# Four-layer hybrid decoder trunk on one core: some low weight parts by an accumulating DMA, and conditioning tiles dealt anew

## The chip, the cores and the metric

The program runs on one core of a Trainium2 chip. The metric is the device time of one execution in microseconds (us), lower is better. TensorE multiplies matrices (PE in the profile, PEld for its weight loads), VectorE (DVE) and ScalarE (ACT) work on tiles element by element, GpSimd (POOL) fills constants and can issue DMAs, SyncE (SP) issues nearly all DMAs, in the order of its queue.

## What is computed

One sequence of 256 tokens, 1024 wide, passes four layers. Each layer is a token mixer and a gated feed-forward network; both sit behind a normalization that is shifted and scaled by six vectors per layer, made from one conditioning vector `c`.

```python
for i in range(4):
    mod = silu(c) @ ada_w[i] + ada_b[i]                  # 6 x 1024
    sh1, sc1, g1, sh2, sc2, g2 = split(mod, 6)
    h = rmsnorm(x, mix_norm_g[i]) * (1 + sc1) + sh1
    y = [gmlp, mla, hgrn2][i % 3](h)                     # layers 0 and 3: gMLP, 1: attention, 2: recurrence
    x = x + (1 + g1) * y
    h = rmsnorm(x, ffn_norm_g[i]) * (1 + sc2) + sh2
    a = h @ w_up                                         # 1024 x 5632
    gate, val = split(causal_conv3(a) + conv_b, 2)
    x = x + (1 + g2) * ((silu(gate) * val) @ w_down)     # 2816 x 1024
return rmsnorm(x, final_g)
```

All inputs are float32. The recurrence (layer 2) projects `h` to a forget gate f, a query q, a value i and an output gate g, each 1024 wide, and to an output o.

## The kernel before

**Weights.** Every weight passes once through SBUF, in units of 1 MB (128 partitions x 2048 floats, tile `raw`, a ring of five). A unit is converted in two halves of 1024 columns: ACT copies the half to a rounded high part `wh` (L214), DVE subtracts it from the raw half to get the low part `wl` (L217); seven halves of each are held. Activations are split in the same way (`hh` and `hlo` behind a norm, `gh` and `gl` in the feed-forward network). Each product is three matmuls: high x high, high x low, low x high.

`unit()` is called where a stage takes its next weight unit. It first issues the DMAs of coming units, then converts as far ahead as it should: three units as a rule, two in the out-projections, and three again at an out-projection's last unit, so that the first two units behind a norm are converted ahead of the norm (`LAST = 3`). `state["chain"]` puts later conversions behind the norm's own chain.

**A norm between two stages.** The end of an out-projection (`dn` of the feed-forward network, `go` of gMLP, `wo` of the others) is `out_end`: DVE multiplies by the gate (`early`, then four times `gated`, L541) and adds to `x` (L542), ACT sums squares, a root and a reciprocal follow, `gx` is the scaled `x` (L477, L480, L481). PE turns it into `xt` (L489), ACT and DVE make `hh` (L503) and `hlo` (L510, L514) with the shift and scale of the conditioning (`mod`, `amul`). `early` is put behind the last low part that DVE has made (`state["sub"]`) and behind the last conditioning tile on DVE.

**Conditioning.** `mod` of a layer has six parts (l, u): u = 0, 1, 2 are shift, scale and gate of the mixer, 3, 4, 5 those of the feed-forward network. The first two parts of layer 0 are made at the start. The other 22 are dealt to two engines, each part as four 1 MB tiles `adaw` (name: layer, part, quarter). Those in `ADA_P` are sixteen-pass matmuls on PE into `adaps` (L331), which DVE transposes and stores (`adat` L298, `mod` L300, `amul` L266); those in `ADA_D` are two DVE reductions a tile (L356). `RATE` gives for each stage how many tiles of PE and of DVE are loaded per weight unit. `GAPS` and `GAPRUN` say how many tiles for PE are held ready for a norm and are run there, where PE has little else; `HGF` is the number run in the recurrence's out-projection. `need()` runs what a norm or a gate cannot do without. Loads go through SP's queue, among those of the weights; the tiles for DVE and some of those for PE take slots of the `raw` ring.

**Order.** Each engine works through its own queue in order. The order is a scheduler's, made from the program order, priorities and `issue_after`.

Of the kernel before, what the change touches and what calls it, by code (L numbers as in the profile page):

```python
# [8 lines left out]
F32 = mybir.dt.float32  # L9
# [4 lines left out]
ALU = mybir.AluOpType  # L14
# [6 lines left out]
L = 4  # L21
# [3 lines left out]
NF = 22  # L25
GI = 2048
NRAW = 5
GAPS = [2, 4, 3, 3, 1, 2, 2, 0]
GAPRUN = [2, 2, 3, 3, 1, 2, 2]
GAPW = 7  # L30
GAPBIG = 3
LAST = 3
# [9 lines left out]
OLAG = 1  # L42
ROPE = 1
MLA_ADA = (2, 4, 6)
HGF = 2
HGO = "o0 o1 s0 a0 o2 s1 a1 n0 o3 s2 n1 w0 s3 n2 w1 n3 w2 w3"
HOLD = (3, 4)
ADA_P = [(0, 5), (1, 2), (1, 3), (2, 2), (2, 3), (2, 4), (3, 5)]
ADA_D = [(0, 2), (0, 3), (0, 4), (1, 0), (1, 1), (1, 4), (1, 5), (2, 0), (2, 1), (2, 5), (3, 0), (3, 1), (3, 2), (3, 3),
         (3, 4)]  # L50
RATE = {("mix", 0): (0.05, 0.9), ("u", 0): (0.1, 0.8), ("go", 0): (0.35, 0.6), ("up", 0): (0.1, 0.23),
        ("dn", 0): (0.0, 0.65), ("mix", 1): (2.0, 0.0), ("up", 1): (0.0, 0.2), ("dn", 1): (0.0, 0.85),
        ("mix", 2): (0.0, 0.0), ("lev", 2): (0.5, 0.0), ("hout", 2): (0.25, 0.0), ("up", 2): (0.0, 0.2),
        ("dn", 2): (0.0, 0.8), ("mix", 3): (0.0, 0.6), ("u", 3): (0.0, 0.5), ("go", 3): (0.0, 0.7),
        ("up", 3): (0.0, 0.0), ("dn", 3): (0.0, 0.0)}
MAGIC = 12582912.0
TWO_PI = 2.0 * math.pi
# [35 lines left out]
def build(ctx, tc, A, out, stages=None):  # L93
    nc = tc.nc
    pe, act, dve, pool = nc.tensor, nc.scalar, nc.vector, nc.gpsimd
# [60 lines left out]
    i = act.activation(cact[:], cin[:], AF.Silu)  # L156
# [12 lines left out]

    plan = []  # L170

    def want(aps):
        plan.extend(aps)

    state = {"dma": 0, "conv": 0, "use": 0, "ahead": 3, "chain": (), "behind": (), "manual": False, "left": 99, "tag": "raw", "p": 0.0, "d": 0.0, "gap": 0, "rate": {"p": 0.0, "d": 0.0}}
    raws = []
# [1 line left out]
    halves = []  # L178

    def dma_next():  # L180
        ap, n = plan[state["dma"]]
        raw = wp.tile([P, 2048], F32, tag="raw", name=f"raw{state['dma']}", bufs=NRAW)
        state["dma"] += 1
        if state["dma"] == 1:

            nc.sync.dma_start(raw[:, :1024], ap[:, :1024])
            raw_, ap = raw[:, 1024:], ap[:, 1024:]
        else:
            raw_ = raw[:, :n]
        i = nc.sync.dma_start(raw_, ap)  # L190
        state["lastdma"] = getattr(i, "ins", i)
        raws.append((raw, n))

    def conv_half():

        if not halves:
            if state["dma"] == state["conv"]:
                if state["dma"] == len(plan):
                    return
                dma_next()  # L200
            raw, n = raws.pop(0)
            ready.append([])
            halves.extend((raw, o, min(1024, n - o), state["conv"]) for o in range(0, n, 1024))
            state["conv"] += 1
        raw, o, w, n = halves.pop(0)
        wh = wp.tile([P, 1024], F32R, tag="wh", name=f"wh{n}_{o}", bufs=7)
        wl = wp.tile([P, 1024], F32R, tag="wl", name=f"wl{n}_{o}", bufs=7)
        with contextlib.ExitStack() as es:

            for ins in state["chain"]:  # L210
                es.enter_context(tc.issue_after(ins))
            if n == 0 and o and "first" in state:
                es.enter_context(tc.issue_after(state["first"][1]))
            act.copy(wh[:, :w], raw[:, o : o + w])  # L214
            if n == 0 and "first" in state:
                es.enter_context(tc.issue_after(state["first"][0]))
            i = dve.tensor_tensor(wl[:, :w], raw[:, o : o + w], wh[:, :w].bitcast(F32), op=ALU.subtract)  # L217
            state["sub"] = getattr(i, "ins", i)
        ready[-1].append((wh, wl))

    def unit(ahead=None, more=DMA_AHEAD):
# [11 lines left out]
    def pace(kind, l, left=None, tag=None):  # L233
        state["rate"] = dict(zip("pd", RATE[kind, l]))
        state["gap"] = GAPS[2 * l + (kind in ("up", "dn"))]
        if left is not None:
            state["left"] = left
        if tag is not None:
            state["tag"] = tag
# [67 lines left out]
    def ada_tile(name, shape):  # L307
        if state["tag"] == "big":
            return big(name, shape)
        return wp.tile(list(shape), F32, tag="raw", name=name, bufs=NRAW)  # L310

    def ada_tensor(l, u):


        def load(i):
            raw = ada_tile(f"adaw{l}_{u}_{i}", (P, 2, 4, 256))
            nc.sync.dma_start(raw[:].rearrange("p a b c -> p (a b c)"), A["adap"][ADA_P.index((l, u)), i])

            def run():
                h = ADA_P.index((l, u)) % 2  # L320
                ps = adaps[:, h, :]
                if i == 0 and pend[h] in late:
                    late.remove(pend[h])
                    pend[h][1]()
                with contextlib.ExitStack() as es:
                    for ins in state["behind"]:
                        es.enter_context(tc.issue_after(ins))
                    for k in range(2):
                        kc = 2 * i + k
                        for j in range(4):  # L330
                            pe.matmul(ps[32 * j : 32 * j + 32, :], crep(kc), raw[:, k, j, :], start=kc == 0, stop=kc == KC - 1,  # L331
                                      tile_position=(0, 32 * j))
                if i == 3:
                    pend[h] = (state["use"], lambda: mod_store(l, 8 * u, 8, ps), (l, u))
                    late.append(pend[h])
# [5 lines left out]
    def ada_vector(l, u):  # L341
# [62 lines left out]
    def ada_run(m):  # L404
        if not loaded[m]:
            ada_load(m)
        if loaded[m]:
            loaded[m].pop(0)[1]()
            owner[m].pop(0)
# [57 lines left out]
    def root(t, sd):  # L467

        i = dve.reciprocal(sd[:, t : t + 1], sd[:, t : t + 1])
        state["chain"] = (getattr(i, "ins", i),)  # L470
        return sd[:, t : t + 1]

    def scaled(t, rs):

        xn = cur["gx"][:, t, :]
        if t == 0:
            dve.tensor_scalar_mul(xn, x[:, t, :], rs)  # L477
            return
        for o in (0, 256):
            dve.tensor_scalar_mul(xn[:, o : o + 256], x[:, t, o : o + 256], rs)  # L480
        i = act.activation(xn[:, 512:D], x[:, t, 512:D], AF.Copy, scale=rs)  # L481
        state["chain"] += (getattr(i, "ins", i),)
# [35 lines left out]
    def modulated(l, which):  # L518
# [248 lines left out]
    def gmlp_units(j):  # L767
        want([(A["gmv"][j, i], 2048) for i in range(8)])
        want([(A["gmu"][j, i], 2048) for i in range(8)])
        want([(A["gmo"][j, i], 2048) for i in range(8)])  # L770
# [310 lines left out]

    def hg_units():
        for n in ("hg_f", "hg_q", "hg_i", "hg_g", "hg_o"):
            want([(A[n][i], 2048) for i in range(4)])

    def hg_bounds():
        lbp = prm[:, col("lb") : col("lb") + 32].rearrange("p (d h) -> p d h", d=4)
# [23 lines left out]
    def hgrn(l):  # L1111
# [176 lines left out]
        for step in HGO.split():  # L1288
            {"o": recur, "s": root, "n": normed, "w": wo.step, "a": lambda i: ada_run("p") if i < HGF else None}[step[0]](int(step[1]))

# [7 lines left out]
            nc.sync.dma_start(convs[l][:], A["cwb"][l])  # L1298

    def ffn_units(l):  # L1300
        want([(A["up"][l, i], 2048) for i in range(NF)])
        want([(A["dn"][l, i], 2048) for i in range(NF // 2)])

    def ffn(l):
# [34 lines left out]
    for kind, l in stages:  # L1339
        if kind == "mix":  # L1340
            if l % 3 == 0:
                gmlp_units(l // 3)
            elif l == 1:
                mla_units()
            else:
                hg_units()
        elif kind == "ffn":
            ffn_units(l)
# [85 lines left out]
def pack(i):  # L1434
# [23 lines left out]
    def rng(a, n):  # L1458
# [66 lines left out]
```

## Time and profile before

| | |
|---|---|
| median of three runs | 1356.75 us (1356.7 to 1356.93) |
| the profiled execution | 1358.56 us, of which the profile's span is 1356.8 us |
| mean granted TensorE clock | 0.991 |
| PE busy | 1320.5 us (97%) |
| DVE, ACT busy | 1129.1 us (83%), 782.9 us (58%) |
| HBM read | 328.01 MB, 243 GB/s over the span |
| low parts on DVE (L217) | 418 of 1231 ns |
| high parts on ACT (L214) | 418 of 1050 ns |
| conditioning on DVE (L356) | 120 of 1280 ns |

A row of the timeline holds start and length in us, engine, line, operation, what is written from what, and in brackets how long the engine had been idle and who ended that. A row of the windows view holds a stretch of time, its length, then for each engine the busy time and (x) the number of instructions, the granted TensorE clock, the busy share of the DMA engines and GB/s.

### The profile page before, as it was taken

Reading aid. Unit: us, or ns where it says so; the run is one execution under the profiler, and the core shown is the slowest. Engines: PE = TensorE matmul, PEld = TensorE weight load, DVE = VectorE, ACT = ScalarE, POOL = GpSimd, SP = SyncE. Lnnn points to the kernel's source line nnn. Section 1 sums busy time; section 2 is a strip of 40 time slices with the busy share of each in tenths; the row PEclk is TensorE's granted clock in tenths of the full one; section 3 lists DMA queues with packets and bytes.
Section 4 is the critical chain, followed back from the end, with each engine's and each line's share of the span. In section 5 each row is a group of like instructions: output and inputs, shape, how many; then the busy total and the mean of one; then the engine's idle time right before and its main releaser. Section 6 shows DMA issues by size and latency. Waiting matters only on the chain. (4 is left out here: it accounts for less than half of the span.)

```text
span 1356.8 us, 25080 instructions
## 1 busy us (share of the span) xinstructions
PE 1320.5 (97%) x10197; PEld 1200.1 (88%) x10197; DVE 1129.1 (83%) x1865; ACT 782.9 (58%) x1230; POOL 20.0 (1%) x29
## 2 busy tenths in 40 slices
PE   9999999999979999999999999999999999999997
PEld 7799889997768799997897979999778998999986
DVE  5699979889776679999978967899988896888874
ACT  4664466665266566654585547666455753766642
POOL 0100000000000000000010000000001000000000
PEclk9999999999989999999999999999999999999999
DMA  9978955666985355579665364567968588355550
GB/s 380 357 266 312 397 205 214 257 218 232 394 325 203 125 187 202 200 303 372 249 221 199 109 261 156 187 217 280 372 255 338 198 326 330 122 172 178 198 198 32
DMA packets 49308, 330.71 MB, mean 244 GB/s; under 512 B 6565, under 2 KB 7717, under 8 KB 10407
## 3 DMA queue, kind: packets, MB, share of 16 engines
q1 hardware_dynamic: 48032, 326.95, 64.3%
q10 hardware_dynamic: 1160, 2.17, 0.5%
q8 instruction: 80, 1.31, 0.4%
q14 instruction: 36, 0.29, 0.1%
HBM read 328.01 MB, written 1.08 MB: 243 GB/s over the span
## 5 line engine op out<-in xcount | busy, mean ns | idle before, releaser
L214 ACT CAST wh<-raw 128x1024 fp32r<-128x1024 f32 x418 | 428.9, 1050 | 324.2 <-PE up L700 94.5
L217 DVE TENSOR_TENSOR wl<-raw,wh 128x1024 fp32r<-128x1024 f32 x418 | 506.9, 1231 | 93.4 <-ACT wh L214 88.7
L699 PE MATMUL up<-hh,wh 128*128 128x256 f32 x1280 | 314.3, 283 | 0.0
L700 PE MATMUL up<-hlo,wh 128*128 128x256 f32 x1280 | 314.1, 283 | 0.0
L699 PEld LDWEIGHTS up<-hh,wh 128*128 128x128 f32 x1280 | 245.7, 192 | 0.8 <-ACT gh L647 0.4
L700 PEld LDWEIGHTS up<-hlo,wh 128*128 128x128 f32 x1280 | 245.7, 192 | 0.0
L703 PE MATMUL up<-hh,wl 128*128 128x256 f32 x1280 | 179.7, 283 | 0.0
L703 PEld LDWEIGHTS up<-hh,wl 128*128 128x128 f32 x1280 | 165.1, 192 | 0.0
L356 DVE CUSTOM_DVE_ANT_0 adaw<-adaw,cbc,prm 128x1024 f32<-128x1024 f32 x120 | 151.3, 1280 | 3.9 <-DMA adaw<-adad 3.8
L1318 ACT ACTIVATE y<-up,cwb 128x256 f32<-128x256 f32 x176 | 98.8, 562 | 69.6 <-DVE y L1320 69.6
L248 PE MATMUL dn<-wl,gh 128*128 128x512 f32 x339 | 133.5, 394 | 1.5 <-DVE wl L217 1.5
L247 PE MATMUL dn<-wh,gh 128*128 128x512 f32 x339 | 130.2, 390 | 4.1 <-DVE y L1320 2.7
L249 PE MATMUL dn<-wh,gl 128*128 128x512 f32 x339 | 131.2, 390 | 0.0
L1319 DVE SCALAR_TENSOR_TENSOR y<-up,cwb,y 128x255 f32<-128x255 f32 x176 | 84.5, 480 | 29.8 <-ACT y L1318 29.0
L1320 DVE SCALAR_TENSOR_TENSOR y<-up,cwb,y 128x254 f32<-128x254 f32 x176 | 84.2, 478 | 1.8
L247 PEld LDWEIGHTS dn<-wh,gh 128*128 128x128 f32 x339 | 63.7, 188 | 18.5 <-ACT warm L624 3.5
L248 PEld LDWEIGHTS dn<-wl,gh 128*128 128x128 f32 x339 | 63.6, 188 | 18.4 <-DVE wl L217 5.7
L249 PEld LDWEIGHTS dn<-wh,gl 128*128 128x128 f32 x339 | 63.6, 188 | 12.8
L699 PE MATMUL u<-hh,wh 128*128 128x256 f32 x256 | 64.6, 290 | 0.0
L700 PE MATMUL u<-hlo,wh 128*128 128x256 f32 x256 | 62.8, 283 | 0.0
L648 DVE TENSOR_TENSOR gl<-g,gh 128x256 fp32r<-128x256 f32 x88 | 37.1, 421 | 19.3 <-ACT gh L647 18.0
L552 ACT ACTIVATE gated<-x 128x512 f32<-128x512 f32 (+1 forms) x40 | 21.8, 545 | 52.9 <-DVE x L542 50.4
(383 smaller groups left out, 2234.6 us busy)
## 6 DMA issues: line engine op xcount, KB each, us to landing
raw<-up SPq DMA_DIRECT2D x88, 1024.0 KB
adaw<-adad SPq DMA_DIRECT2D x60, 1024.0 KB
raw<-dn SPq DMA_DIRECT2D x44, 1024.0 KB
adaw<-adap SPq DMA_DIRECT2D x28, 1024.0 KB
raw<-gmu SPq DMA_DIRECT2D x16, 1024.0 KB
raw<-gmo SPq DMA_DIRECT2D x16, 1024.0 KB
raw<-gmv SPq DMA_DIRECT2D x15, 1024.0 KB
adaf<-ada SPq DMA_DIRECT2D x7, 1024.0 KB
```

The costliest lines, as they stand in the source:

```text
L214: act.copy(wh[:, :w], raw[:, o : o + w])
L217: i = dve.tensor_tensor(wl[:, :w], raw[:, o : o + w], wh[:, :w].bitcast(F32), op=ALU.subtract)
L247: pe.matmul(ps, lh, rh, start=start, stop=False)
L248: pe.matmul(ps, lh, rl, start=False, stop=False)
L249: i = pe.matmul(ps, ll, rh, start=False, stop=stop)
L356: r = dve.tensor_tensor_reduce(raw[:, e, :], raw[:, e, :], cbc[:], 1.0, prm[:, c0 : c0 + 1], ALU.mult, ALU.add, mod[:, l, b : b + 1])
L699: pe.matmul(ps[:, g, :], a, src_h(k), start=k == 0, stop=False)
L700: pe.matmul(ps[:, g, :], a, src_l(k), start=False, stop=False)
L703: i = pe.matmul(ps[:, g, :], b, src_h(k), start=False, stop=k == nk - 1)
L1318: act.activation(y[:], ps[:, e, :], AF.Identity, bias=b, scale=w[2])
L1319: dve.scalar_tensor_tensor(y[:, 1:], ps[:, e, : S - 1], w[1], y[:, 1:], op0=ALU.mult, op1=ALU.add)
L1320: dve.scalar_tensor_tensor(y[:, 2:], ps[:, e, : S - 2], w[0], y[:, 2:], op0=ALU.mult, op1=ALU.add)
```

## The change

Two things are changed. For some units (0 and 1 of each `up`, 0 and 1 of the recurrence's `hg_f`, all four of `hg_i` and of `hg_g`) the first half's low part isn't made by DVE any more: ACT writes the negated high part into `wl`, and a DMA that POOL issues reads the same 512 KB of the weight again from HBM and adds it. These are 18 of 418 halves. `early` now follows the last low part that is still DVE's.

The conditioning tiles are dealt anew. Parts (1,1) and (1,4) move from DVE to PE, (0,5) and (2,2) from PE to DVE; there are still 28 tiles for PE and 60 for DVE. One tile of layer 2 is run in the gap behind its recurrence and no more in the out-projection (`HGF`, `GAPS`, `GAPRUN`), and the loading rates differ.

```diff
-GAPS = [2, 4, 3, 3, 1, 2, 2, 0]
-GAPRUN = [2, 2, 3, 3, 1, 2, 2]
+GAPS = [2, 4, 3, 3, 2, 2, 2, 0]
+GAPRUN = [2, 2, 3, 3, 2, 2, 2]
...
-HGF = 2
+HGF = 1
...
-ADA_P = [(0, 5), (1, 2), (1, 3), (2, 2), (2, 3), (2, 4), (3, 5)]
...
+ADA_P = [(1, 1), (1, 2), (1, 3), (1, 4), (2, 3), (2, 4), (3, 5)]
+ADA_D = [(l, u) for l in range(L) for u in range(6) if (l, u) > (0, 1) and (l, u) not in ADA_P]
-RATE = {("mix", 0): (0.05, 0.9), ("u", 0): (0.1, 0.8), ("go", 0): (0.35, 0.6), ("up", 0): (0.1, 0.23),
-        ("dn", 0): (0.0, 0.65), ("mix", 1): (2.0, 0.0), ("up", 1): (0.0, 0.2), ("dn", 1): (0.0, 0.85),
...
+RATE = {("mix", 0): (0.05, 0.9), ("u", 0): (0.1, 0.85), ("go", 0): (0.35, 0.4), ("up", 0): (0.1, 0.2),
+        ("dn", 0): (0.0, 0.4), ("mix", 1): (2.0, 0.0), ("up", 1): (0.0, 0.26), ("dn", 1): (0.0, 0.9),
...
-    def want(aps):
-        plan.extend(aps)
+    def want(aps, again=()):
+        plan.extend((*a, i in again) for i, a in enumerate(aps))
...
+        again = plan[n][2] and o == 0
...
-            i = dve.tensor_tensor(wl[:, :w], raw[:, o : o + w], wh[:, :w].bitcast(F32), op=ALU.subtract)
-            state["sub"] = getattr(i, "ins", i)
+            if again:
+                act.mul(wl[:, :w], raw[:, o : o + w], -1.0)
+                pool.dma_start(wl[:, :w], plan[n][0][:, o : o + w], accum_op=ALU.add)
+            else:
+                i = dve.tensor_tensor(wl[:, :w], raw[:, o : o + w], wh[:, :w].bitcast(F32), op=ALU.subtract)
+                state["sub"] = getattr(i, "ins", i)
...
-            want([(A[n][i], 2048) for i in range(4)])
+            want([(A[n][i], 2048) for i in range(4)], {"hg_f": (0, 1), "hg_i": range(4), "hg_g": range(4)}.get(n, ()))
...
-        want([(A["up"][l, i], 2048) for i in range(NF)])
+        want([(A["up"][l, i], 2048) for i in range(NF)], (0, 1))
```

SP's queue at the end of layer 0's down-projection, in front of the attention's first weights (`raw56` is the last unit of `dn`, `adaw1_4_1` quarter 1 of part (1,4)). Before:

```order
L190 DMA raw55_3881<-dn 128x2048
L317 DMA adaw1_2_3_3893<-adap 128x2048
L347 DMA adaw1_1_2_3628<-adad 128x2048
L347 DMA adaw1_1_3_3700<-adad 128x2048
L347 DMA adaw1_4_0_3736<-adad 128x2048
L317 DMA adaw1_2_0_3775<-adap 128x2048
L347 DMA adaw1_4_1_3813<-adad 128x2048
L317 DMA adaw1_2_1_3815<-adap 128x2048
L347 DMA adaw1_4_2_3853<-adad 128x2048
L317 DMA adaw1_2_2_3855<-adap 128x2048
L190 DMA raw56_3919<-dn 128x2048
L347 DMA adaw1_4_3_3931<-adad 128x2048
```

And of the change, at the same place:

```order
L190 DMA raw55_3873<-dn 128x2048
L353 DMA adaw1_0_1_3661<-adad 128x2048
L353 DMA adaw1_0_2_3767<-adad 128x2048
L323 DMA adaw1_2_0_3769<-adap 128x2048
L323 DMA adaw1_2_1_3805<-adap 128x2048
L353 DMA adaw1_0_3_3845<-adad 128x2048
L323 DMA adaw1_2_2_3847<-adap 128x2048
L323 DMA adaw1_2_3_3883<-adap 128x2048
L190 DMA raw56_3909<-dn 128x2048
L190 DMA raw57_3947<-mla_a 128x2048
L190 DMA raw58_3969<-mla_a 128x2048
```

Seven conditioning tiles stand between the last two units of `dn` where nine stood, and none where one stood behind `raw56`.

DVE's queue at the end of layer 0's `go`, ahead of the norm of the feed-forward network (`wl23` belongs to `go`, `wl24` and `wl25` to the two `up` units behind the norm). Before:

```order
L217 TENSOR_TENSOR wl23_1024_1760<-raw23_1714,wh23_1024_1759 128x1024
L217 TENSOR_TENSOR wl24_0_1782<-raw24_1753,wh24_0_1781 128x1024
L217 TENSOR_TENSOR wl24_1024_1786<-raw24_1753,wh24_1024_1785 128x1024
L217 TENSOR_TENSOR wl25_0_1790<-raw25_1777,wh25_0_1789 128x1024
L217 TENSOR_TENSOR wl25_1024_1794<-raw25_1777,wh25_1024_1793 128x1024
L541 TENSOR_TENSOR early_1798<-go3_1535,gx_1638 128x512
```

And of the change:

```order
L223 TENSOR_TENSOR wl23_1024_1758<-raw23_1712,wh23_1024_1757 128x1024
L223 TENSOR_TENSOR wl24_1024_1783<-raw24_1751,wh24_1024_1782 128x1024
L223 TENSOR_TENSOR wl25_1024_1792<-raw25_1773,wh25_1024_1791 128x1024
L547 TENSOR_TENSOR early_1796<-go3_1535,gx_1638 128x512
L548 TENSOR_TENSOR x_69<-x_69,early_1796 128x512
```

Two of the four low parts ahead of `early` are gone from DVE; the last of them stays.

DVE's queue in the norm ahead of layer 1's `up`, where (1,4) is the scale of that very norm. Before:

```order
L480 TENSOR_SCALAR gx_4858<-x_69,ss_5003 128x256 x2
L510 TENSOR_SCALAR nt_5121<-xt_5085,amul_90,mod_89 128x256
L510 TENSOR_SCALAR nt_5130<-xt_5088,amul_90,mod_89 128x256
L514 TENSOR_TENSOR hlo_93<-nt_5121,hh_92 128x256
L514 TENSOR_TENSOR hlo_93<-nt_5130,hh_92 128x256
```

And of the change:

```order
L486 TENSOR_SCALAR gx_4843<-x_69,ss_4990 128x256 x2
L304 STREAM_TRANSPOSE adat_5107<-adaps_91 128x256
L306 TENSOR_TENSOR mod_89<-adat_5107,prm_70 128x8
L272 SCALAR_TENSOR_TENSOR amul_90<-mod_89,prm_70 128x8
L516 TENSOR_SCALAR nt_5112<-xt_5072,amul_90,mod_89 128x256
L516 TENSOR_SCALAR nt_5121<-xt_5075,amul_90,mod_89 128x256
```

Between `gx` and the first `nt`, DVE now turns and stores what PE has just made for part (1,4).

More of the change, by code (lines that the diff above doesn't have):

```diff
@@ L44 @@
 MLA_ADA = (2, 4, 6)
-HGF = 2
+HGF = 1
 HGO = "o0 o1 s0 a0 o2 s1 a1 n0 o3 s2 n1 w0 s3 n2 w1 n3 w2 w3"
 HOLD = (3, 4)
-ADA_P = [(0, 5), (1, 2), (1, 3), (2, 2), (2, 3), (2, 4), (3, 5)]
-ADA_D = [(0, 2), (0, 3), (0, 4), (1, 0), (1, 1), (1, 4), (1, 5), (2, 0), (2, 1), (2, 5), (3, 0), (3, 1), (3, 2), (3, 3),
-         (3, 4)]
-RATE = {("mix", 0): (0.05, 0.9), ("u", 0): (0.1, 0.8), ("go", 0): (0.35, 0.6), ("up", 0): (0.1, 0.23),
-        ("dn", 0): (0.0, 0.65), ("mix", 1): (2.0, 0.0), ("up", 1): (0.0, 0.2), ("dn", 1): (0.0, 0.85),
-        ("mix", 2): (0.0, 0.0), ("lev", 2): (0.5, 0.0), ("hout", 2): (0.25, 0.0), ("up", 2): (0.0, 0.2),
-        ("dn", 2): (0.0, 0.8), ("mix", 3): (0.0, 0.6), ("u", 3): (0.0, 0.5), ("go", 3): (0.0, 0.7),
+ADA_P = [(1, 1), (1, 2), (1, 3), (1, 4), (2, 3), (2, 4), (3, 5)]
+ADA_D = [(l, u) for l in range(L) for u in range(6) if (l, u) > (0, 1) and (l, u) not in ADA_P]
+RATE = {("mix", 0): (0.05, 0.9), ("u", 0): (0.1, 0.85), ("go", 0): (0.35, 0.4), ("up", 0): (0.1, 0.2),
+        ("dn", 0): (0.0, 0.4), ("mix", 1): (2.0, 0.0), ("up", 1): (0.0, 0.26), ("dn", 1): (0.0, 0.9),
+        ("mix", 2): (0.0, 0.0), ("lev", 2): (0.5, 0.3), ("hout", 2): (0.25, 0.0), ("up", 2): (0.0, 0.2),
+        ("dn", 2): (0.0, 0.75), ("mix", 3): (0.0, 0.5), ("u", 3): (0.0, 0.6), ("go", 3): (0.0, 0.55),
         ("up", 3): (0.0, 0.0), ("dn", 3): (0.0, 0.0)}
@@ L180, in dma_next @@
     def dma_next():
-        ap, n = plan[state["dma"]]
+        ap, n, _ = plan[state["dma"]]
         raw = wp.tile([P, 2048], F32, tag="raw", name=f"raw{state['dma']}", bufs=NRAW)
```

## Prediction

> **What bounds the kernel now.** I read the busy times first, then who PE waited for, then stretches of time around the norms, then the rows of single stalls.
>
> ```profile
> PE 1320.5 (97%) x10197; PEld 1200.1 (88%) x10197; DVE 1129.1 (83%) x1865; ACT 782.9 (58%) x1230; POOL 20.0 (1%) x29
> PE xt L489 <- DVE gx L477: 7.4, 2, 6.9
> 169.80:178.00 8.20, 5.05 (x49) 3.89 (x49) 7.08 (x20) 6.25 (x18) 0.00 (x0) 0.84 0.79 329
> 372.20:384.40 12.20, 5.26 (x49) 4.09 (x49) 10.74 (x26) 7.77 (x19) 0.00 (x0) 0.69 1.00 422
> 469.50:475.00 5.50, 5.37 (x66) 3.27 (x65) 4.52 (x15) 4.22 (x13) 0.00 (x0) 1.00 0.00 0
> 664.10:668.50 4.40, 4.40 (x65) 3.13 (x65) 3.30 (x12) 3.40 (x11) 0.00 (x0) 1.00 0.02 4
> 1157.40:1161.50 4.10, 3.58 (x48) 2.59 (x48) 3.09 (x11) 3.19 (x10) 0.00 (x0) 1.00 0.00 0
> ```
>
> PE is busy 97%, and its matmuls are the same after the change: 28 conditioning tiles on PE before and after, no product added. So time can only come out of PE's gaps. The second line (engine, who released it, us in all, times, the longest) says that of the norms' transposes one waited 6.9 us for `gx`. The other lines are stretches from the last out-projection matmul to the first product behind a norm (length; busy PE, PEld, DVE, ACT, POOL; granted clock; DMA share; GB/s). Most last 4 to 5.5 us. Two stand out: the feed-forward norm of layer 0 (8.2 us, clock 0.84, DMA 0.79) and the norm ahead of the attention (12.2 us, clock 0.69, DMA 1.00). Both long gaps have a full DMA, the short ones an empty one. In both it is not the arithmetic of the norm that is late, but the weights converted ahead of it.
>
> **The change: layer 0's feed-forward norm.**
>
> ```profile
> 152.90 2.81 SPq L190 DMA_DIRECT2D raw<-up  x2
> 160.66 2.00 ACT L214 CAST wh<-raw 128x1024 fp32r<-128x1024 f32 x2 [1.24 <-DMA raw<-up]
> 163.09 2.00 ACT L214 CAST wh<-raw 128x1024 fp32r<-128x1024 f32 x2 [0.42 <-DMA raw<-up]
> 161.75 4.79 DVE L217 TENSOR_TENSOR wl<-raw,wh 128x1024 fp32r<-128x1024 f32 x4 [0.89 <-ACT wh L214]
> 166.46 0.68 DVE L541 TENSOR_TENSOR early<-go,gx 128x512 f32<-128x512 f32 x1
> 173.94 0.75 DVE L477 TENSOR_SCALAR gx<-x,ss 128x1024 f32<-128x1024 f32 x1
> 340.00:350.00 10.00, 10.00 (x46) 8.29 (x45) 9.18 (x13) 2.59 (x4) 0.00 (x0) 1.00 1.02 429
> ```
>
> `early` starts when the fourth low part ends, and `gx` follows 7.48 us later. ACT waits for the raw weights; one conversion is 1.0 us, one low part 1.2. A tile of 1.05 MB takes 2.44 us of a full DMA (last line, 429 GB/s). The order of the changed kernel has one conditioning tile less ahead of these units, so they land near 158.2. ACT then has six operations instead of four (two negated copies join, priced like a cast): 158.2, with the second unit there by 160.6, so about 164.2; one low part behind it, 165.4. `early` is 1.1 us sooner. If the DMA relief fails, ACT's six from 160.66 end at 166.7, the low part at 167.9: 1.4 us later. If ACT's copies are hidden, the DMA's whole 2.4 us come through. **Gain 1.1** (−1.4 to 2.4): nearest to the rows as they chain.
>
> **The attention's norm.**
>
> ```profile
> 361.75 1.99 ACT L214 CAST wh<-raw 128x1024 fp32r<-128x1024 f32 x2 [16.14 <-DMA raw<-dn]
> 362.84 0.51 PE L247 MATMUL dn<-wh,gh 128*128 128x512 f32 x1 [1.38 <-ACT wh L214]
> 364.10 0.50 PE L248 MATMUL dn<-wl,gh 128*128 128x512 f32 x1 [0.76 <-DVE wl L217]
> 369.14 2.00 ACT L214 CAST wh<-raw 128x1024 fp32r<-128x1024 f32 x2 [0.44 <-DMA raw<-mla_a]
> 367.79 4.80 DVE L217 TENSOR_TENSOR wl<-raw,wh 128x1024 fp32r<-128x1024 f32 x4
> 372.50 0.68 DVE L541 TENSOR_TENSOR early<-dn,gx 128x512 f32<-128x512 f32 x1
> 380.25 0.75 DVE L477 TENSOR_SCALAR gx<-x,ss 128x1024 f32<-128x1024 f32 x1
> 381.06 3.71 PE L489 MATMUL xt<-ident,gx 128*128 128x128 f32 x16 [6.94 <-DVE gx L477]
> 384.00:386.00 2.00, 2.00 (x11) 2.00 (x10) 2.00 (x6) 2.00 (x6) 0.00 (x0) 0.50 0.97 410
> 1159.84 1.95 PE L489 MATMUL xt<-ident,gx 128*128 128x128 f32 x16 [0.52 <-DVE ss L469]
> ```
>
> The last `dn` unit lands so late that ACT sat 16.14 us and PE stalled twice; the attention's units land at 366.7 and 369.1, and their low parts hold `early` until 372.50. SP's queue held nine conditioning tiles ahead of that last unit and one behind; the change has seven and none. At 2.44 us each, the last unit comes 4.9 us sooner and the attention's 7.3. PE's two stalls go, and with the slower starts beside them about 2.9 us (1.38 + 0.76 + 0.8 by start-to-start times of those matmuls): the tail ends at 369.3 instead of 372.2. The last high part starts at 361.8, `early` follows at 364.9 (3.1 behind, a little under the 3.36 of before, since the low parts queue less), `gx` 7.75 later at 372.65, `xt` at 373.5. That is 4.1 us behind the tail. `xt` takes 1.95 us at full clock (last line) or 3.71 at half, so products start at 375.4 or 377.2 against 384.4. I take the middle, 8.1 us sooner, and 0.4 us for part of the half-clock stretch 384 to 386, which costs 1.0. **Gain 8.5**; half clock throughout gives 7.2, full clock 10.0, and only the shorter tail with a partly shorter wait about 5. What is late next: `gx`, still, by a little.
>
> **Starts of the down-projections.**
>
> ```profile
> 618.22 0.47 PE L247 MATMUL dn<-wh,gh 128*128 128x512 f32 x1 [1.36 <-DVE y L1320]
> 962.98 0.47 PE L247 MATMUL dn<-wh,gh 128*128 128x512 f32 x1 [1.35 <-DVE y L1320]
> 644.55 1.28 DVE L356 CUSTOM_DVE_ANT_0 adaw<-adaw,cbc,prm 128x1024 f32<-128x1024 f32 x1
> ```
>
> PE waits for DVE's last `y`. Layer 2's `up` gets eight conditioning reductions ahead of it instead of twelve, 5.1 us less for DVE, more than the 1.35. Layer 1's has as many as before or one less. **Gain 1.6** (0.5 to 3): the whole of layer 2's stall and 0.25 of layer 1's.
>
> **What it costs.**
>
> ```profile
> 474.99 0.37 PE L687 MATMUL up<-hh,wh 128*128 128x256 f32 x1
> 473.15 1.06 PE L331 MATMUL adaps<-adaw,cact 128*32 128x256 f32 x14
> 472.60 1.93 ACT L503 ACTIVATE hh<-xt,mod,amul 128x256 fp32r<-128x256 f32 x4
> 816.56 0.45 DVE L298 STREAM_TRANSPOSE adat<-adaps 128x256 f32<-128x256 f32 x1
> 817.04 0.17 DVE L300 TENSOR_TENSOR mod<-adat,prm 128x8 f32<-128x8 f32 x1
> 817.90 0.15 DVE L266 SCALAR_TENSOR_TENSOR amul<-mod,prm 128x8 f32<-128x8 f32 x1
> 658.14 0.68 DVE L541 TENSOR_TENSOR early<-dn,gx 128x512 f32<-128x512 f32 x1
> 818.06 1.94 PE L489 MATMUL xt<-ident,gx 128*128 128x128 f32 x16 [1.57 <-DVE amul L266]
> ```
>
> In layer 1's feed-forward norm the scale (1,4) now comes from PE, whose last conditioning run there begins at 473.15 and ends at 474.21. `hh`, which ACT began at 472.60, must wait for it: DVE's turn, store and scale (0.45 + 0.17 + 0.15) end at 474.98, the first of four `hh` takes 1.93 / 4 = 0.48, so the first product starts at 475.46 instead of 474.99. Queued behind those three on DVE are `nt` and `hlo`, for which PE's product of the low activations waits. **Cost 0.5** (0, if the tile comes earlier in the run, to 2, if `hlo` is late too). Ahead of the recurrence's norm (`early` at 658.14, tail end 664.1, both balanced), layer 1's `dn` has sixteen reductions instead of twelve, 5.1 us, less two low parts, 2.4: `early` may be 2.7 later, of which most fits in the 6 us to the tail. **Cost 0.5** (0 to 2.7). In the recurrence DVE loses eight low parts (9.6 us) and gains three tiles (7.7), ACT gains eight copies (8.4), PE is nearly full there: 0 ± 1.5; without that cover, a part of ACT's 8.4 us would stand ahead of the gates that it makes there. One tile more is run in layer 2's gap, 1.1 us, inside the 1.57 us idle of the last row: 0. The other norms lose DVE work of which the tail was as late: 0. Copies at 18 x 1.0 us on ACT, busy 58%, are hidden elsewhere, as are 9.4 MB read again, with the DMA empty at the short norms.
>
> **Sum:** 1.1 + 8.5 + 1.6 − 0.5 − 0.5 = 10.2 us. The profiled execution takes 1358.56 us (its span 1356.8 and 1.8 around it), so 1348.4 of its kind; it lies 1.8 above the median, for which I forecast 1356.75 − 10.2 = **1346.5**. Most of it is the new deal; the low parts by DMA bring about 1 us by themselves.
>
> **Rivals.** *The clock stays full in both shortened gaps.*
>
> ```profile
> 744.18 0.60 PE L1150 MATMUL gram<-qk 128*32 128x32 f32 x47 [2.29 <-issue]
> 815.40:819.70 4.30, 2.73 (x32) 2.07 (x32) 3.47 (x14) 3.20 (x10) 0.00 (x0) 1.00 0.02 4
> 746.00:748.00 2.00, 2.00 (x10) 2.00 (x11) 2.00 (x3) 0.00 (x0) 0.00 (x0) 0.50 1.06 332
> ```
>
> An idle time of 2.29 us was followed by half clock two us later, one of 1.57 (the row at 818.06, in the stretch 815.4 to 819.7) by none. The new gaps leave PE idle some 2.4 us at once (the attention's 4.1 us behind the tail less two conditioning runs there of 0.8 to 1.1 us each): just above the one that lost it. If it stays, the attention's gain is 10.0 instead of 8.5, and layer 0's norm saves 8.2 x 0.16 = 1.3: **1343.7**. The Trainium skill ("TensorE: Matmul & The Clock Gate", Part 1) has the clock halve after an idle window of about 3.4 us, by which both gaps would keep it. The trace disagrees, with half clock behind 2.29 us.
>
> *The deal does not bring the attention's weights forward*, since the ring of five, or DVE's release of its slots, holds them and not the DMA. For it: ACT's 16.14 us idle would look the same. Against it: DMA at 1.00 to 1.02. Then 1.1 + 1.6 − 1.0 = 1.7 us: **1355.0**.
>
> *The accumulating DMA is late (slower).*
>
> ```profile
> 1149.22 1.05 ACT L214 CAST wh<-raw 128x1024 fp32r<-128x1024 f32 x1 [1.67 <-PE go L249]
> 1161.74 0.28 PE L688 MATMUL up<-hh,wl 128*128 128x256 f32 x1
> ```
>
> No such DMA is in the trace. At one end, 0.52 MB at 429 GB/s take 1.2 us, or 2.4 if the destination is read too. At the other, an `up` unit issued at 152.90 was converted at 160.66, 7.8 us, in a full DMA. A norm has two on POOL's queue, the second copied by ACT near 1148.6 and needed at 1161.74: 13.1 us. At 7.8 each, one behind the other, 15.6 us are 2.5 too long at each of five norms (four `up`, one `hg_f`): 12.5 us, more than the gain, **1359.0**, and up to 1368 if each `xt` falls to half clock (1.8 x 5). It decides from 13.1 us a pair and turns the sign at 13.1 + 10.2 / 5 = 15.1. POOL's 20.0 us of work speak against a queue. I take 3 us, nearest the first end, since the norms' DMA is empty. The Trainium skill ("SBUF — State Buffer", SBUF: two separate sides) says that a DMA issued by GpSimd has descriptors written by GpSimd, which some copies on VectorE lock out, and gives 620 ns that became 3100; that ratio on 1.2 us makes, as an estimate, 12 us a pair, just under what decides. No run here shows it yet.
>
> **How the numbers follow.** Forecast 0.64, full clock 0.13, deal without effect 0.12, late DMA 0.11. The parts' bounds around the forecast are about 1340 to 1353; with some of the third case I end at 1354.5, and leave out 0.19: the rest of that case and the late DMA. About 0.2%, 2.7 us, is what a measurement of this kernel can tell from no change. Faster by more (below 1354.0): 0.64 + 0.13 and a little of the third case, 0.79; slower by more (above 1359.5): most of the last, 0.10; between: 0.11.
>
> **What would show it.** Right: `early` of the attention's norm near 365 and its gap 6 to 8 us; no stall of PE at the last `dn` unit; `early` of layer 0's norm near 165.4; no wait for `y` at layer 2's `dn`. Wrong: a wait of PE for `wl` by a DMA behind a norm; `early` near 372; the recurrence longer by over 2 us; layer 1's norm over 6 us.

## The result, and the profile after

The change makes the kernel slower: 1363.1 us median (1358.38 to 1365.36, 17 runs) against 1357.77 (1356.15 to 1360.62, 17 runs) for the kernel before in the same sessions, a ratio of 1.0034 (95% interval 1.0025 to 1.0044). The forecast was 1346.5, and the range ended at 1354.5. The profiled execution takes 1361.2 us, its span 1359.5, against 1358.56 and 1356.8.

From the page of the change, the busy times and two rows of the DMA queues (packets, MB, share of the time of 16 engines):

```profile
PE 1318.8 (97%) x10197; PEld 1198.6 (88%) x10197; DVE 1108.9 (82%) x1847; ACT 798.4 (59%) x1248; POOL 38.0 (3%) x47
...
q1 hardware_dynamic: 48032, 326.95, 64.3%
q0 software_dynamic: 2592, 9.44, 3.8%
```

DVE has 20 us less work and ACT 16 more, near what 18 halves moved from one to the other come to (22 at 1.23 us, 19 at 1.05); POOL's queue q0 is new, with 9.44 MB. Then the first rows of what PE waited for (line numbers lie six above those of before):

```profile
PE psum L1165 <- DVE hsg L1181: 8.1, 1, 8.1
PE gram L1156 <- issue: 6.9, 2, 3.6
PE xt L495 <- DVE gx L483: 3.6, 3, 1.7
```

The wait for `gx` that led before (6.9 us at the attention) is gone. A wait that was not there at all leads now: 8.1 us for `hsg`, in the recurrence, and `gram` beside it has two gaps where it had one of 2.29. The norms, in windows of the change (columns as before): layer 0's feed-forward norm, the attention's, the recurrence's.

```profile
169.80:175.80 6.00, 3.88 (x51) 2.66 (x49) 4.95 (x15) 4.76 (x14) 0.00 (x0) 1.00 1.03 340
366.60:372.70 6.10, 4.37 (x50) 3.09 (x49) 4.92 (x15) 5.57 (x14) 0.00 (x0) 0.92 1.02 430
652.40:658.70 6.30, 4.82 (x67) 3.18 (x65) 5.26 (x17) 4.93 (x14) 0.00 (x0) 1.00 0.84 272
```

The attention's gap is 6.1 us instead of 12.2, layer 0's 6.0 instead of 8.2, both with more clock; the recurrence's grew from 4.4 to 6.3, now with a DMA that is busy. Timeline rows of the first two:

```profile
165.53 0.68 DVE L547 TENSOR_TENSOR early<-go,gx 128x512 f32<-128x512 f32 x1
361.74 0.68 DVE L547 TENSOR_TENSOR early<-dn,gx 128x512 f32<-128x512 f32 x1
370.29 2.77 PE L495 MATMUL xt<-ident,gx 128*128 128x128 f32 x16 [1.71 <-DVE gx L483]
```

`early` comes 0.9 and 10.8 us sooner than before, and `xt` at the attention 10.8. To find where the time went I take the first matmul of each stage in both traces. Lengths in us, worked out from those starts, one execution of each kernel (the last two columns are experiments below; `q` is a product some 20 us into the attention):

| from ... to | before | change | deal alone | tiles earlier |
|---|---|---|---|---|
| start to `up` of layer 0 | 178.0 | 175.8 | 177.3 | 175.9 |
| to the attention's `q` | 226.6 | 217.1 | 216.0 | 218.6 |
| to `up` of layer 1 | 70.4 | 71.0 | 71.3 | 71.0 |
| to the recurrence's first product (`hf`) | 193.5 | 194.8 | 193.7 | 196.0 |
| to `hi` | 46.2 | 46.2 | 46.2 | 46.9 |
| to `gram` | 25.2 | **35.6** | 26.9 | 25.2 |
| to the gates (`g`) | 22.8 | **26.9** | 22.3 | 24.3 |
| to `up` of layer 2 | 57.1 | 56.9 | 56.9 | 59.4 |
| to layer 3's first product | 192.9 | 191.7 | 191.7 | 191.7 |
| to the end | 344.2 | 343.5 | 343.5 | 343.4 |

At the recurrence's start the change is 9.8 us ahead (668.5 against 658.7). In the 48 us from `hi` to the gates it loses 14.5, and the later stages give 2.1 back: 1359.5 against 1356.8 at the end. So the miss lies in two rows of this table. Timeline rows of the change in the first of them, in order of time, on POOL, SP, DVE and PE:

```profile
695.66 0.88 POOL L221 DMA_DIRECT2D wl<-hg_i  x1 [2.53 <-PE hq L706]
700.12 0.69 DVE L1181 TENSOR_TENSOR hsg<-hq,hk 128x512 f32<-128x512 f32 x1
700.13 0.33 SPq L353 DMA_DIRECT2D adaw<-adad  x1
701.46 0.87 POOL L221 DMA_DIRECT2D wl<-hg_i  x1 [4.91 <-PE hq L706]
711.77 1.28 DVE L362 CUSTOM_DVE_ANT_0 adaw<-adaw,cbc,prm 128x1024 f32<-128x1024 f32 x1 [8.27 <-DMA adaw<-adad]
714.18 0.68 DVE L1181 TENSOR_TENSOR hsg<-hq,hk 128x512 f32<-128x512 f32 x1
714.92 1.93 PE L1165 MATMUL psum<-hsg,ones 128*32 128x512 f32 x8 [8.09 <-DVE hsg L1181]
```

And two windows there:

```profile
695.00:712.00 17.00, 11.84 (x92) 11.15 (x90) 5.16 (x7) 9.58 (x11) 2.60 (x3) 0.93 1.04 315
...
712.00:720.00 8.00, 5.08 (x16) 2.74 (x17) 5.84 (x8) 1.04 (x1) 0.00 (x0) 0.50 0.80 241
```

The conditioning tile that the deal puts here is issued by SP at 700.13 and lands only at 711.77. DVE's queue has its two reductions ahead of the fourth `hsg`, so DVE sits idle for 8.27 us with `hsg` behind it. PE's queue has `psum`, which reads `hsg`, ahead of most of `hi`, so PE sits idle for 8.09 us with products behind it; and the clock is 0.50 from 712 to 720. From `hi` to `gram` the change takes 10.4 us more than before.

The theory to test (A): the accumulating DMAs fill the DMA there, and by that the tile is late. Its main rival (B): the tile would stall DVE there without them.

### The profile page after: what moved, and what is told of

The parts are those of the page before. It is cut to its first block, busy times and chain, and to the rows that moved or that the text cites. A ratio compares the mean times of both kernels' runs of the same rounds, so it can differ in the third digit from the quotient of the medians.

```text
span 1359.5 us, 25127 instructions
## 1 busy us (share of the span) xinstructions
PE 1318.8 (97%) x10197; PEld 1198.6 (88%) x10197; DVE 1108.9 (82%) x1847; ACT 798.4 (59%) x1248; POOL 38.0 (3%) x47
## 3 DMA queue, kind: packets, MB, share of 16 engines
q1 hardware_dynamic: 48032, 326.95, 64.3%
q0 software_dynamic: 2592, 9.44, 3.8%
q8 instruction: 80, 1.31, 0.4%
## 4 chain that ended last, share of the span: by engine, by line
PE 72%; DVE 13%; DMA 6%; ACT 5%; issue 4%; SPq 0%; ACTq 0%; DVEq 0%
PE up L705 11%; PE up L706 11%; PE up L709 11%; PE dn L254 4%; PE dn L255 4%; PE dn L253 4%; DVE wl L223 3%; DVE adaw L362 2%; ACT wh L215 2%; DVE x L548 2%; DMA adaf<-ada 1%; PE v L750 1%; DMA adaw<-adad 1%; DVE gated L547 1%; PE up L693 1%
## 5 line engine op out<-in xcount | busy, mean ns | idle before, releaser
L223 DVE TENSOR_TENSOR wl<-raw,wh 128x1024 fp32r<-128x1024 f32 x400 | 485.5, 1229 | 96.8 <-ACT wh L215 96.3
L255 PEld LDWEIGHTS dn<-wh,gl 128*128 128x128 f32 x339 | 63.6, 188 | 13.1
L653 ACT CAST gh<-g 128x256 fp32r<-128x256 f32 x88 | 35.3, 401 | 30.0 <-DVE g L1331 29.5
```

Source lines behind the costliest of these rows:

```text
L255: i = pe.matmul(ps, ll, rh, start=False, stop=stop)
```

## The experiments

Times are medians; the kernel before, measured beside each group, took 1357.7, 1358.3 and 1357.0 us.

**The two halves of the change.** The first kernel keeps the deal and makes all low parts on DVE:

```diff
-            want([(A[n][i], 2048) for i in range(4)], {"hg_f": (0, 1), "hg_i": range(4), "hg_g": range(4)}.get(n, ()))
+            want([(A[n][i], 2048) for i in range(4)], ())
...
-        want([(A["up"][l, i], 2048) for i in range(NF)], (0, 1))
+        want([(A["up"][l, i], 2048) for i in range(NF)], ())
```

> The new deal, no low part by DMA (all 418 on DVE). Theory A (in the recurrence the accumulating DMAs, 2.9 us of full DMA each by the queue's share, fill the DMA, so that a conditioning tile lands late, DVE holds hsg behind it and PE waits 8.1 us; gram's instruction gap grows with the same load): the recurrence takes as long as before within 2 us, about 1347 us against 1357. Theory B (the two conditioning tiles for DVE that the deal puts into the recurrence stall it by themselves): PE's wait for hsg stays at 6 us or more and the time is 1355 or above.

Measured: 1346.48 us, ratio 0.9919 (0.9893 to 0.9946). The second keeps the old tables and adds the low parts by DMA; as a diff against the change:

```diff
-GAPS = [2, 4, 3, 3, 2, 2, 2, 0]
+GAPS = [2, 4, 3, 3, 1, 2, 2, 0]
...
-ADA_P = [(1, 1), (1, 2), (1, 3), (1, 4), (2, 3), (2, 4), (3, 5)]
+ADA_P = [(0, 5), (1, 2), (1, 3), (2, 2), (2, 3), (2, 4), (3, 5)]
...
-        ("mix", 2): (0.0, 0.0), ("lev", 2): (0.5, 0.3), ("hout", 2): (0.25, 0.0), ("up", 2): (0.0, 0.2),
+        ("mix", 2): (0.0, 0.0), ("lev", 2): (0.5, 0.0), ("hout", 2): (0.25, 0.0), ("up", 2): (0.0, 0.2),
...
```

> The old deal with the 18 low parts by DMA. Theory A: slower than before by the fetch gaps in gram (some 5 us) but without the 8 us for hsg, as no conditioning tile for DVE is loaded there: 1358 to 1363. Theory B: the low parts cost nothing, 1355 to 1357.

Measured: 1361.91 us, ratio 1.0030 (1.0017 to 1.0043). The wait for `hsg` isn't there: from `hi` to `gram` it takes 25.2 us as before. So the deal alone brings the time that was forecast, the low parts alone cost some 4 us, and with the new deal they cost 16. In the timeline of the deal alone stand the same instructions of SP and DVE:

```profile
699.80 0.33 SPq L353 DMA_DIRECT2D adaw<-adad  x1
704.73 1.28 DVE L362 CUSTOM_DVE_ANT_0 adaw<-adaw,cbc,prm 128x1024 f32<-128x1024 f32 x1 [1.63 <-DMA adaw<-adad]
```

And the same window:

```profile
695.00:712.00 17.00, 15.32 (x109) 13.26 (x108) 15.01 (x19) 7.29 (x9) 0.00 (x0) 1.00 0.79 295
```

The tile is issued at 699.80 instead of 700.13 and is there at 704.73 instead of 711.77: seven us sooner, with the DMA busy 0.79 of the 17 us instead of all of it. DVE waits 1.63 us for it even so. Theory B holds for that much, some 1.7 us, and A for the rest.

**Low parts by DMA behind the norms only:**

```diff
-            want([(A[n][i], 2048) for i in range(4)], {"hg_f": (0, 1), "hg_i": range(4), "hg_g": range(4)}.get(n, ()))
+            want([(A[n][i], 2048) for i in range(4)], {"hg_f": (0, 1)}.get(n, ()))
```

> The change with the low parts by DMA only behind the norms (up units 0 and 1, hg_f 0 and 1), those of hg_i and hg_g on DVE again. Theory A: the recurrence is as long as before, about 1346 to 1348, with no wait of PE for hsg over 1 us. Theory B: as the change, 1360 or above.

Measured: 1349.25 us, 0.9938 (0.9916 to 0.9960); PE waits 2.1 us for `hsg`, 27.3 us from `hi` to `gram`. That is 1.3 us above what A said, with a wait of twice the length it allowed, near the 1.7 of the deal alone. The norms do not carry the loss.

**No conditioning tile for DVE in the levels:**

```diff
-        ("mix", 2): (0.0, 0.0), ("lev", 2): (0.5, 0.3), ("hout", 2): (0.25, 0.0), ("up", 2): (0.0, 0.2),
+        ("mix", 2): (0.0, 0.0), ("lev", 2): (0.5, 0.0), ("hout", 2): (0.25, 0.0), ("up", 2): (0.0, 0.2),
```

> The change without conditioning tiles for DVE in the recurrence's levels (rate 0.3 to 0; two tiles of part (2,2) are loaded later, in the out-projection). Theory A: the 8 us wait for hsg goes, gram's two gaps stay, so about 1362 less 10 (the wait and the half clock behind it), 1351 to 1354. Theory B: all of the loss goes, 1346 to 1349. A third, that the accumulating DMAs hold hi's or hg's products directly: no better than the change, 1360 or above.

Measured: 1365.75 us, 1.0060 (1.0037 to 1.0083): by the time, the third theory. By the stages it isn't: from `hi` to `gram` 25.2 us, the wait gone as A has it. The two tiles belong to (2,2), the gate of the recurrence's out-projection. They arrive later instead, so that `early` has to wait for the gate and layer 2's feed-forward norm is held up in turn:

```profile
813.77 0.69 DVE L547 TENSOR_TENSOR early<-wo,gx 128x512 f32<-128x512 f32 x1 [4.59 <-DMA gx<-gate]
822.28 3.65 PE L495 MATMUL xt<-ident,gx 128*128 128x128 f32 x16 [5.31 <-DVE amul L272]
```

From the gates to `up` of layer 2 it takes 66.3 us instead of 56.9. The experiment moved the stall, and could not decide by its time. So the **fifth** kernel moves the tiles **earlier**, all 18 low parts by DMA:

```diff
-        ("mix", 2): (0.0, 0.0), ("lev", 2): (0.5, 0.3), ("hout", 2): (0.25, 0.0), ("up", 2): (0.0, 0.2),
+        ("mix", 2): (0.0, 0.3), ("lev", 2): (0.5, 0.0), ("hout", 2): (0.25, 0.0), ("up", 2): (0.0, 0.2),
```

> The change with all its 18 low parts by DMA, and the conditioning tiles for DVE loaded and reduced among the recurrence's f and q projections instead of its levels (rate of the levels 0.3 to 0, of the projections 0 to 0.3; three tiles are loaded a few places earlier). If DVE's hold behind the late tile makes the 8 us: no wait for hsg, hi to gram 25 to 26 us instead of 35.6, and the time 9 to 12 below the change's 1363, 1351 to 1354. If the accumulating DMAs cost those 10 us in any order: 1360 or above.

Measured: 1351.69 us, 0.9952 (0.9935 to 0.9969), no wait for `hsg`, 25.2 us from `hi` to `gram` (last column of the table). The same DMAs, the same reductions, three tiles a few places further ahead in SP's queue: 11 us. That settles A for the larger part: it takes both, the load on the DMA and a consumer of a loaded tile ahead of `hsg`. What is left stands behind `gram`: from there to `up` of layer 2 (two rows of the table, between which the products of `hg` fall differently here) it takes 83.7 us, in the change 83.8, in the deal alone 79.2.

**Which low parts.** Those of `hg_i` without `hg_g`'s, then the other way round, the norms' kept:

```diff
-            want([(A[n][i], 2048) for i in range(4)], {"hg_f": (0, 1), "hg_i": range(4), "hg_g": range(4)}.get(n, ()))
+            want([(A[n][i], 2048) for i in range(4)], {"hg_f": (0, 1), "hg_i": range(4)}.get(n, ()))
```

```diff
-            want([(A[n][i], 2048) for i in range(4)], {"hg_f": (0, 1), "hg_i": range(4), "hg_g": range(4)}.get(n, ()))
+            want([(A[n][i], 2048) for i in range(4)], {"hg_f": (0, 1), "hg_g": range(4)}.get(n, ()))
```

> The change with hg_g's low parts on DVE again, hi's four by DMA. If the loss at hi comes from those four alone (their DMAs delay the conditioning tile for DVE): from the first product of hi to gram 33 to 36 us as in the change, from gram to the gates 22 to 24 as without them; time 1356 to 1360. If the low parts of hg_g are what fills the DMA there: hi to gram near 27, time near 1349.

> The change with hg_i's low parts on DVE again, hg_g's four by DMA. If the load of DMAs lengthens gram's gaps: hi to gram near 27 us, gram to the gates 25 to 27, PE's gaps in gram two and over 5 us in all; time 1350 to 1354. If gram's gaps have nothing to do with them: 22 to 23 from gram to the gates, time near 1348.

Measured: 1357.44 us (0.9995, 0.9986 to 1.0005) with `hg_i`'s, 35.2 us to `gram` and 22.2 to the gates; 1355.73 (0.9975, 0.9965 to 0.9986) with `hg_g`'s, 27.3 and 26.7, the time 1.7 above what was expected. Two losses, then, each with its own four DMAs: the tile with `hi`'s, and `gram`'s gaps with `hg_g`'s. The rows of those gaps in the timeline of the change:

```profile
745.74 0.60 PE L1156 MATMUL gram<-qk 128*32 128x32 f32 x47 [3.30 <-issue]
753.39 0.97 PE L1156 MATMUL gram<-qk 128*32 128x32 f32 x80 [3.60 <-issue]
```

Of the deal alone:

```profile
735.47 0.60 PE L1156 MATMUL gram<-qk 128*32 128x32 f32 x47 [2.13 <-issue]
```

Of the kernel with `hg_g`'s:

```profile
738.85 0.60 PE L1156 MATMUL gram<-qk 128*32 128x32 f32 x47 [3.10 <-issue]
746.50 1.07 PE L1156 MATMUL gram<-qk 128*32 128x32 f32 x80 [2.12 <-issue]
```

With `hg_g`'s DMAs the two gaps are 3.10 and 2.12 us, with `hg_i`'s 2.31 and 1.31, with the norms' alone 2.11 and 1.57. So of the 4.4 us that `hg_g`'s cost from `gram` to the gates against the norms' alone, the gaps themselves are 1.5. The rest goes with the clock, which falls to half behind each of the two gaps, and behind none with the norms' alone. Two windows of the kernel with `hg_g`'s:

```profile
740.17:743.58 3.41, 3.41 (x19) 3.25 (x15) 3.41 (x4) 0.98 (x1) 0.00 (x0) 0.50 0.79 145
747.00:750.41 3.41, 3.41 (x59) 3.35 (x47) 2.04 (x3) 2.00 (x2) 0.00 (x0) 0.50 0.04 14
```

**Adding or copying.** The DMA writes instead of adding, so the low part is the whole weight and the addition is left out:

```diff
-                pool.dma_start(wl[:, :w], plan[n][0][:, o : o + w], accum_op=ALU.add)
+                pool.dma_start(wl[:, :w], plan[n][0][:, o : o + w])
```

> The change with the DMA writing instead of adding (the low part is then the whole weight: the addition of the negated high part is left out). If adding is what makes these DMAs long (2.9 us of full DMA each against 1.2 for the bytes), they land in 3 to 6 us instead of 5.6 to 11.4, the conditioning tile lands 3 to 4 us after its 704.73 of the deal alone or sooner, PE's wait for hsg is under 4 us, and the time 1349 to 1355. If it is the bytes or POOL's queue: as the change, 1359 or above.

Measured: 1355.11 us, 0.9977 (0.9966 to 0.9989), a little above what the first case said and far below the second, as are its other signs (they land in 6.4 us, PE waits 4.25). From the list of DMAs (count, KB each, median us from issue to landing) and of queues, of the change:

```profile
q0 software_dynamic: 2592, 9.44, 3.8%
...
wl<-hg_i POOLq DMA_DIRECT2D x4, 512.0 KB, 10.1
```

Of the copying kernel:

```profile
q0 software_dynamic: 2592, 9.44, 2.1%
...
wl<-hg_i POOLq DMA_DIRECT2D x4, 512.0 KB, 6.4
```

And its timeline at the tile:

```profile
700.88 0.33 SPq L353 DMA_DIRECT2D adaw<-adad  x1
708.68 1.28 DVE L362 CUSTOM_DVE_ANT_0 adaw<-adaw,cbc,prm 128x1024 f32<-128x1024 f32 x1 [4.43 <-DMA adaw<-adad]
711.83 1.94 PE L1165 MATMUL psum<-hsg,ones 128*32 128x512 f32 x8 [4.25 <-DVE hsg L1181]
```

From its issue to DVE's start on it the tile takes 4.93 us with no low part by DMA, 7.80 with copies, 11.64 with additions. Somewhat under half of the delay is the second read and POOL's queue, which no run took apart; the rest is the adding.

**Low parts by DMA for `up` alone:**

```diff
-            want([(A[n][i], 2048) for i in range(4)], {"hg_f": (0, 1), "hg_i": range(4), "hg_g": range(4)}.get(n, ()))
+            want([(A[n][i], 2048) for i in range(4)], ())
```

> The change with low parts by DMA only for the first two units of each up, none in the recurrence. By the stages so far: layer 0's norm 1.3 us shorter than with the deal alone, the recurrence's norm 1.4 shorter than with hg_f's low parts, the rest equal: about 1345, within 2 us of the deal alone (1346.5). A rival, that low parts behind the norms cost something by themselves: 1348 or above.

Measured: 1347.82 us, 0.9917 (0.9902 to 0.9933). Beside the deal alone's 0.9919 this is neither gain nor loss that can be measured. Of the two parts expected one shows: from `up` of layer 1 to `hf` it takes 193.2 us, with `hg_f`'s low parts 195.1. Layer 0's norm isn't shorter: `up` starts at 177.1, in the deal alone at 177.3.

**The main term by itself**, the deal alone with one rate as before:

```diff
-        ("dn", 0): (0.0, 0.4), ("mix", 1): (2.0, 0.0), ("up", 1): (0.0, 0.26), ("dn", 1): (0.0, 0.9),
+        ("dn", 0): (0.0, 0.65), ("mix", 1): (2.0, 0.0), ("up", 1): (0.0, 0.26), ("dn", 1): (0.0, 0.9),
```

> The deal alone, with the rate of conditioning tiles in layer 0's down-projection as before (0.4 to 0.65). If the gain at the attention's norm comes from fewer tiles of SP's queue at the end of that stage: from the start of dn to the first product of the attention 94 to 98 us (before 97.1, deal alone 86.9), time 1353 to 1357. If it comes from the dealing of (1,1) and (1,4) to PE and not from the rate: 86 to 89 us and about 1347.

Measured: 1355.05 us, 0.9985 (0.9975 to 0.9994); 95.2 us from the start of `dn` to `q` (which is what the expectation calls the attention's first product), PE waiting 6.87 us for `gx` again. Of the 10 us or so that the deal brings, this one number brings 8.6.

**A version without the loss:** the first kernel's edit (no low parts by DMA) and the fifth's (tiles earlier) together.

> The same move of three tiles without low parts by DMA. The deal alone lost 1.7 us from hi to gram (a wait of 1.7 for hsg); this should go: about 1345, at most 2 below the deal alone (1346.5). A rival: the tiles only move the wait into the projections, 1347 or above.

Measured: 1345.98 us, 0.9913 (0.9898 to 0.9928), 25.9 us from `hi` to `gram`, with a wait of 0.7 for `hsg` left. With the deal alone it is the fastest here; between the two the measurement doesn't tell.

## Why the prediction was wrong

The step that failed is the recurrence's: "In the recurrence DVE loses eight low parts (9.6 us) and gains three tiles (7.7), ACT gains eight copies (8.4), PE is nearly full there: 0 ± 1.5". It counted DVE, ACT and PE, and not the DMA. The re-reads were covered by "9.4 MB read again, with the DMA empty at the short norms", but eight of the eighteen are not at a norm: they lie between `hi` and the gates. And of the three tiles "gained" it counted DVE's 7.7 us of work, not what queues behind a tile that is not there. It cost 14.5 us where 0 was said. Of the signs set down for being wrong, the recurrence that is longer by over 2 us is this one.

Beneath it lies a size: "I take 3 us, nearest the first end, since the norms' DMA is empty", with 1.2 us of DMA each. The medians to landing are 8.9 to 10.3 us, by group. By the queue's row each takes 0.038 x 1359.5 / 18 = 2.9 us of all 16 engines; the same bytes at q1's rate take 0.643 x 1359.5 / 326.95 x 0.524 = 1.4, and the copies of the experiment 0.021 x 1354.7 / 18 = 1.6. The end of 7.8 us, which I put into the rival, was nearer, and still low.

The rival of the late DMA had the right cause and the wrong place. It set the price at the norms, two DMAs one behind the other against 13.1 us. They overlap: POOL issues the second without waiting for the first, and with the low parts at the norms alone the loss isn't there. The change was slower by a wait that no rival named. The Trainium skill ("SBUF — State Buffer", SBUF: two separate sides), which the prediction named beside that rival, would have some of DVE's copies lock out GpSimd's writing of descriptors; here DVE was idle from 703.5 to 711.77 while the one issued at 701.46 was under way, and by the trace it landed 10.3 us after its issue. So that lock does not explain its length.

The other terms, by the stages of the change:

- Layer 0's feed-forward norm: 1.1 said, 2.2 measured; `early` at 165.53 (165.4 said). But the low parts by DMA did not bring it. With them and the old deal `early` is at 167.63, 1.2 later than before, as the lower bound of this term had it; without them, in the deal with one rate as before, whose `go` starts within 0.2 us of the change's, at 164.92. So what helped is rather the conditioning tile less ahead of these units. The clock stayed at 1.00, as in the rival of the full clock, and that was luck: of the eight kernels with the new deal and these low parts, the change among them, four lost it there.
- The attention's norm: 8.5 said, 9.5 measured, and the rate alone shown to make 8.6. `early` came at 361.74, three us sooner than said (364.9); the clock in the gap was 0.92.
- Starts of the down-projections: layer 2's stall is gone, 1.2 us in its stage; the expected 1.35.
- Layer 1's feed-forward norm cost 0.6 (0.5 said), though its gap is 6.3 us, over the 6 set down as a sign of being wrong. The recurrence's norm with its `dn` cost 1.3 (0.5 said; by the deal alone 0.1). With the new deal and `hg_f`'s low parts by DMA this stage takes 194.8 to 197.2 us, without them 193.2 to 196.1, with them and the old deal 193.6, so they are not the cause by themselves.
- "The low parts by DMA bring about 1 us by themselves": no. They cost 4 us with the old deal, 16 with the new; eight halves at `up` alone cost nothing that can be measured.

The sum of 10.2 us is near what the deal alone brings, 11.2 from the 1357.7 measured beside it, and its main term was right by its mechanism. That its 1346.48 us meets the 1346.5 of the forecast is luck: the kernel before took 1 us more in these sessions than the 1356.75 of the forecast, and the forecast held low parts that the deal alone doesn't have. The low parts by DMA were not weighed as a load at all.

## What to carry to other kernels

A transfer that replaces work on an engine has to be priced on the DMA where it falls, stage by stage, and the first question is who else waits for the DMA there. Work that is "gained" on an in-order engine is priced by what stands behind it when its operand is late, not by its own length. And when an experiment removes a wait, read the stage and not the total: the tile moved later took the wait along to the next norm.

## What the runs showed of the hardware

An adding DMA took 2.9 us of all DMA engines for 0.52 MB, about twice a copy from the same queue (1.6). The Trainium skill ("DMA: Bandwidth & Descriptors", Anatomy of one DMA — SWDGE (gpsimd) path) fits a DMA issued by GpSimd by 2.0 us plus its bytes at 436 GB/s, here an estimate of 3.2 us. Here the copies landed after 6.4 to 9.2 us and the additions after 8.9 to 10.3 (medians by group), beside other loads.

`gram`, of which 207 matmuls start within 2 us, stops behind these 207 (once 208) in every run, and in ten of thirteen again 128 matmuls later, with nothing to wait for that the timeline shows. The page of the change has a queue that holds instructions, 80 packets in the whole run, so 16 KB each. PE's 10197 matmuls and as many weight loads come to 255 for each packet, so that 128 matmuls with their loads use up one:

```profile
q8 instruction: 80, 1.31, 0.4%
```

The single packets of this queue, taken from the traces, show what PE waits for:

| stop of `gram` | PE stops | packet starts, ends | PE goes on |
|---|---|---|---|
| before | 741.89 | 741.47, 742.80 | 744.18 |
| deal alone | 733.34 | 733.04, 734.06 | 735.47 |
| change, first | 742.44 | 743.33, 744.30 | 745.74 |
| change, second | 749.79 | 751.01, 751.90 | 753.39 |
| tiles earlier | 735.46 | 738.03, 738.98 | 740.32 |

In all thirteen traces each such stop of over 1 us, 23 of them, ends 1.2 to 1.6 us after one of these packets has ended. By the traces, then, PE waits for its next instructions here; no run changed the stream of them by itself. The longer stops are those whose packet starts later, while the packet itself takes 0.9 to 1.3 us in all. The first stop lasts 2.1 to 2.4 us in the seven kernels without low parts of `hg_g` by DMA, 2.9 to 4.9 in the five that add them, and 1.65 in the copying one, whose second lasts 3.00. A busy DMA alone does not do it: in five kernels without `hg_g`'s by DMA the share in the 3 us ahead of the second stop is 0.99 to 1.02, from SP's queue, and the stop lasts 1.3 to 1.6 us. Why the packet starts later beside POOL's DMAs is open.

Nor does the length of one idle time decide the clock, as I had taken it from 2.29 us before. By the clock records, each stretch at half clock in the thirteen traces, the cut-off last of each aside, lasts 3.41 us or two or three times that, and within a trace all begin whole multiples of 3.41 us apart. Windows of the change cut along this grid:

```profile
740.42:743.83 3.41, 2.03 (x208) 1.92 (x208) 3.41 (x4) 3.32 (x5) 0.40 (x1) 1.00 0.97 211
743.83:747.24 3.41, 1.50 (x66) 0.97 (x65) 2.39 (x4) 1.09 (x2) 0.47 (x1) 1.00 0.80 271
747.24:750.66 3.42, 2.55 (x64) 2.31 (x63) 3.42 (x5) 1.06 (x1) 0.00 (x0) 1.00 0.87 180
750.66:754.07 3.41, 0.68 (x78) 0.68 (x80) 1.07 (x1) 0.00 (x0) 0.00 (x0) 1.00 0.75 298
754.07:757.48 3.41, 3.41 (x39) 3.35 (x28) 2.32 (x3) 2.00 (x2) 0.00 (x0) 0.50 0.04 14
```

And of the deal alone:

```profile
733.12:736.53 3.41, 1.28 (x88) 1.03 (x78) 3.41 (x5) 1.74 (x2) 0.00 (x0) 1.00 0.36 65
736.53:739.94 3.41, 3.41 (x21) 2.73 (x13) 3.41 (x4) 0.00 (x0) 0.00 (x0) 0.50 0.98 377
```

The change's stop of 3.30 us falls into two windows, which keep PE busy for 2.03 and 1.50 us, and the clock stays; its stop of 3.60 leaves 0.68 in one window, the deal's of 2.13 leaves 1.28, and the next window runs at half clock. Around `gram` the other traces have half clock behind windows at full clock with up to 1.50 us busy and full clock behind some from 1.35, so the border lies near there and is not sharp in the modelled busy time. The Trainium skill ("TensorE: Matmul & The Clock Gate", Part 1) has a window of about 3.4 us that runs by itself, and the traces agree. Its rule asks for a whole idle window, though; here 1.28 us of work in one did not keep the clock.
